# Running sums of squares of all norms: from VectorE to GpSimd

## The chip, the cores and the metric

The kernel runs on one core of a Trainium2 chip. Its metric is the device time of one execution in microseconds (us), the median of several runs. The engines of the core work side by side, each through its own instruction list in order: TensorE (PE in the trace; PEld is its weight load), VectorE (DVE), ScalarE (ACT), GpSimd (POOL) and SyncE (SP, which issues the DMA transfers). An instruction starts when the one before it on its engine has been issued and when the semaphores it waits for have been raised.

## What is computed

One inference step of a hybrid backbone of two layers on 640 tokens (512 latent, 128 context) with 1024 channels. Each layer is FFN, token mixer, FFN; the mixer of the first layer is differential attention, that of the second a gated linear recurrence (HGRN). Every sub-layer normalises its input and its output and adds the result to the residual stream:

```python
def rmsnorm(x, g):
    xf = x.astype(jnp.float32)
    y = xf * lax.rsqrt(jnp.mean(xf * xf, axis=-1, keepdims=True) + EPS)
    return (y * g.astype(jnp.float32)).astype(x.dtype)
def ada_pre(x, mod, j, g):
    return rmsnorm(x, g) * (1 + scale) + shift
def ada_post(x, y, mod, j, g, res_w):
    return x + res_w * gate * rmsnorm(y, g)
def swiglu(h, w_in, w_out):
    a, b = jnp.split(h @ w_in, 2, axis=-1)
    return (jax.nn.silu(a) * b) @ w_out
def ffn_sublayer(x, mod, j, g_pre, g_post, w_in, w_out):
    return ada_post(x, swiglu(ada_pre(x, mod, j, g_pre), w_in, w_out), mod, j, g_post, 0.5)
```

scale, shift and gate are rows of a modulation that is computed from a conditioning vector with matmuls of their own. So six sub-layers hold twelve norms, each over 640 tokens.

## The kernel before

**Layout.** Activations stand with channels on partitions: X, Y and H are arrays of eight tiles of 128 channels by 640 tokens. The tokens are in two groups, 0 and 1, of NG = 320, and each norm is done for each group apart: twelve norms by two groups make 24 norm sums. Most matmuls are 128x128 weights against 320 tokens. Values and weights are split into a high and a low part, whl and H (index 0 and 1), and three products make up one (lines 452, 457 and 484); ScalarE writes the high part of a weight (line 360), VectorE the low one (line 362).

**A norm.** `square` (lines 545 to 556) squares one tile on ScalarE: the first tile's squares are written into the group's running sum acc (line 552), the others into a tile sq of two buffers (line 555), and the function that it returns adds sq to acc (line 556). There are seven such adds for each norm sum. When all eight tiles are in, `stat_mm` (line 522) multiplies acc by ones on TensorE, which sums over the partitions; `token_rstd` and `rsqrt` (lines 529 and 507 to 517) compute the reciprocal root in 13 small instructions on VectorE; `token_spread` (line 534) brings it back to all partitions with matmuls by the identity.

**Who calls it.** At the startup, X is transposed on TensorE (line 855), copied (line 858) and squared tile by tile for both groups; then follow the modulation rows (matmuls of line 763, ScalarE's copy of line 873, matmuls of line 724, VectorE's lines 733 and 748) and the first normalised input. At the end of a sub-layer, `y_part` adds the last part of the output product to a tile of Y (line 1132) and squares it; its add is put into a list (`self.later`), from which the loop over matmul jobs takes one at its next step. `post_gen` does the post norm of a group: the sum, then per tile nt = Y times gate times root (line 573), X += nt (line 579) and the square of X, whose add comes one step later. `pre_gen` sums these squares and writes the normalised input: nt (line 606), the high part of H on ScalarE (line 611), the low part on VectorE (line 619). Both are generators that `run_jobs` steps between the matmuls of the jobs, so that one group's norm runs beside the other group's matmuls. The very last post norm writes the output (`last_out`).

**What sets the order.** The program is written out as above, and the scheduler of the language then places each engine's instructions by its own estimate of when they can run. A change of one instruction's engine therefore moves others on all engines. Each sub-layer's end and the next one's start are called a joint here: A, FFN to attention; B, attention to FFN; C, FFN to FFN of the next layer; D, FFN to HGRN; E, HGRN to FFN. In each joint there are four norm sums, in this order: post norm of group 0, pre norm of group 0, post norm of group 1, pre norm of group 1.

Of the kernel before, what the change touches and what calls it, by code (L numbers as in the profile page):

```python
# [14 lines left out]
ALU = mybir.AluOpType  # L15
# [203 lines left out]
class Net:  # L219
# [328 lines left out]
    def square(self, g, src, first):  # L548
        nc = self.nc
        acc = self.acc[g]  # L550
        if first:
            nc.scalar.activation(out=acc, in_=src, func=AF.Square)
            return lambda: None
        sq = self.np_.tile([128, NG], F32, name="sq", tag="sq", bufs=2)
        nc.scalar.activation(out=sq, in_=src, func=AF.Square)  # L555
        return lambda: nc.vector.tensor_tensor(out=acc, in0=acc, in1=sq, op=ALU.add)  # L556

    def post_gen(self, l, j, g, ps, squares):
        nc = self.nc
# [1168 lines left out]
```

## Time and profile before

| | |
|---|---|
| median of 3 runs | 2783.96 us (2780.76 to 2785.59) |
| the profiled execution's own time | 2780.47 us |
| its span in the profile | 2778.7 us |
| mean granted TensorE clock | 0.990 |
| busy: TensorE, VectorE, ScalarE, GpSimd | 98%, 71%, 47%, 0% of the span |
| the 168 adds of line 556 | 80.1 us on VectorE |

The span runs from the first to the last instruction that the profiler recorded; the time has in addition what lies around it. A row of the timeline has the start and the duration in us, the engine, the line, the operation, what is written and read, how many instructions are merged, and in brackets the idle time before it with what ended that. A duration covers the whole of an instruction, and the next one on the same engine can start before it ends. A row of windows has the busy time of each engine in a stretch with the number of instructions, the granted clock of TensorE as a share, the DMA engines' share and GB/s. A wait row has the total, the times and the longest.

### The profile page before, as it was taken

The numbers are of one execution on the slowest core, as the hardware profiler recorded it, in microseconds if no ns is written. First come the engines' busy times: TensorE is split into PE (matmuls) and PEld (weight loads), VectorE is DVE, ScalarE is ACT, GpSimd is POOL, SyncE is SP. The second block draws the span as 40 slices with busy tenths as digits, with TensorE's granted clock in tenths as the row PEclk, the third lists the DMA queues.
The fourth block names the chain that finished last, engine by engine and source line by source line (L and its number), as shares of the span: only waits on it lengthen the run. The fifth ranks groups of instructions, "written<-read, shape, count | busy, mean of one in ns | idle before, by whom it ended". The sixth has DMA issues, their size and how long they took to land.

```text
span 2778.7 us, 47467 instructions
## 1 busy us (share of the span) xinstructions
PE 2715.6 (98%) x18670; PEld 2613.1 (94%) x18670; DVE 1977.8 (71%) x4285; ACT 1307.3 (47%) x2693; POOL 0.2 (0%) x4
## 2 busy tenths in 40 slices
PE   7999999899999999999999999999999999999998
PEld 5999999899998999999999999999999999999997
DVE  6766676887777965667786657687677678867574
ACT  4443444476675553435354434443343345545363
POOL 0000000000000000000000000000000000000000
PEclk9999999999999999999999999999999999999999
DMA  9556224211122456524244442421221222323231
GB/s 305 176 192 198 81 77 145 60 53 54 46 74 75 161 161 201 165 81 145 69 143 132 142 145 77 137 78 35 61 58 50 60 65 93 90 77 90 78 122 54
DMA packets 426077, 299.10 MB, mean 108 GB/s; under 512 B 9051, under 2 KB 386429, under 8 KB 424829
## 3 DMA queue, kind: packets, MB, share of 16 engines
q1 hardware_dynamic: 425344, 295.86, 34.6%
q8 instruction: 147, 2.41, 0.4%
q14 instruction: 78, 0.63, 0.1%
q10 hardware_dynamic: 508, 0.20, 0.0%
HBM read 280.82 MB, written 15.20 MB: 107 GB/s over the span
## 4 chain that ended last, share of the span: by engine, by line
PE 89%; DVE 5%; ACT 4%; DMA 1%; issue 1%; ACTq 0%; DVEq 0%; SPq 0%
PE mmps L484 31%; PE mmps L452 30%; PE mmps L457 15%; PE aux L1564 2%; PE aux L763 2%; PE mmps L1403 1%; DVE whl L362 1%; PE aux L1372 1%; ACT p L1302 1%; PE aux L1373 1%; PE aux L522 1%; PE aux L1601 1%; PE aux L534 1%; ACT whl L360 1%; ACT sq L1635 0%
## 5 line engine op out<-in xcount | busy, mean ns | idle before, releaser
L360 ACT ACTIVATE whl<-wraw 128x512 fp32r<-128x512 f32 (+4 forms) x644 | 464.2, 722 | 661.3 <-PE mmps L452 369.6
L362 DVE TENSOR_TENSOR whl<-wraw,whl 128x512 fp32r<-128x512 f32 (+4 forms) x644 | 515.3, 801 | 207.8 <-ACT whl L360 199.6
L452 PE MATMUL mmps<-H,whl 128*128 128x320 f32 x2624 | 571.5, 317 | 9.3 <-ACT H L611 6.9
L484 PE MATMUL mmps<-H,whl 128*128 128x320 f32 x3456 | 544.1, 309 | 0.1
L484 PEld LDWEIGHTS mmps<-H,whl 128*128 128x128 f32 x3456 | 515.3, 188 | 10.5 <-issue 4.2
L452 PE MATMUL mmps<-G,whl 128*128 128x320 f32 x2448 | 487.7, 311 | 3.8 <-ACT G L1649 1.5
L452 PEld LDWEIGHTS mmps<-H,whl 128*128 128x128 f32 x2624 | 432.5, 191 | 19.5 <-ACT H L611 8.3
L452 PEld LDWEIGHTS mmps<-G,whl 128*128 128x128 f32 x2448 | 391.2, 188 | 13.7 <-issue 5.9
L457 PE MATMUL mmps<-H,whl 128*128 128x320 f32 x1312 | 369.6, 314 | 0.7 <-DVE whl L362 0.7
L484 PE MATMUL mmps<-T,whl 128*128 128x320 f32 x2160 | 352.5, 309 | 0.0
L484 PEld LDWEIGHTS mmps<-T,whl 128*128 128x128 f32 x2160 | 325.4, 188 | 5.0 <-issue 2.5
L457 PE MATMUL mmps<-G,whl 128*128 128x320 f32 x1224 | 304.9, 310 | 0.0
L457 PEld LDWEIGHTS mmps<-H,whl 128*128 128x128 f32 x1312 | 239.1, 191 | 1.1 <-DVE whl L362 1.0
L457 PEld LDWEIGHTS mmps<-G,whl 128*128 128x128 f32 x1224 | 211.4, 188 | 0.0
L452 PE MATMUL mmps<-G,H 128*128 128x320 f32 x880 | 198.7, 312 | 0.1
L1132 DVE TENSOR_TENSOR Y<-Y,mmps 128x320 f32<-128x320 f32 x208 | 94.8, 482 | 127.8 <-PE mmps L457 127.6
L452 PEld LDWEIGHTS mmps<-G,H 128*128 128x128 f32 x880 | 147.8, 189 | 0.3 <-ACT Y L1130 0.3
L457 PE MATMUL mmps<-G,H 128*128 128x320 f32 x440 | 137.3, 312 | 0.0
L452 PE MATMUL mmps<-H,G 128*128 128x320 f32 x448 | 103.5, 312 | 0.0
L997 ACT ACTIVATE sa<-sa 128x320 f32<-128x320 f32 x144 | 67.9, 471 | 66.4 <-DVE sa L1000 65.5
L135 DVE TENSOR_TENSOR s<-wraw 128x512 f32<-128x512 f32 x72 | 49.7, 690 | 69.0 <-DMA wraw<-in_ffn_w_in 68.9
L556 DVE TENSOR_TENSOR acc<-acc,sq 128x320 f32<-128x320 f32 x168 | 80.1, 485 | 22.1 <-ACT sq L555 21.2
(260 smaller groups left out, 3572.5 us busy)
## 6 DMA issues: line engine op xcount, KB each, us to landing
wraw<-in_ffn_w_in SPq DMA_DIRECT2D x192, 512.0 KB, 4.3
wmod<-in_w_mod SPq DMA_DIRECT2D x66, 1024.0 KB, 7.1
wraw<-in_hgrn_w_in SPq DMA_DIRECT2D x40, 512.0 KB, 3.9
wraw<-in_ffn_w_out SPq DMA_DIRECT2D x32, 448.0 KB, 3.7
wraw<-in_ffn_w_out SPq DMA_DIRECT2D x32, 384.0 KB, 3.3
wraw<-in_attn_w_in SPq DMA_DIRECT2D x24, 512.0 KB, 3.8
xs<-X SPq DMA_DIRECT2D x4, 2560.0 KB, 12.8
wraw<-in_ffn_w_out SPq DMA_DIRECT2D x32, 320.0 KB, 3.2
```

The costliest lines, as they stand in the source:

```text
L135: V.tensor_tensor(out=z, in0=a[:, lo], in1=b[:, lo], op=ALU.subtract)
L360: nc.scalar.activation(out=u.w[0][:, 0:nk, :], in_=src, func=AF.Copy)
L362: self.los.append(lambda: nc.vector.tensor_tensor(out=u.w[1][:, 0:nk, :], in0=src, in1=u.w[0][:, 0:nk, :].bitcast(F32), op=ALU.subtract))
L452: nc.tensor.matmul(out=ps[g][:, 0:NG], lhsT=w[0][:, a, :], rhs=rhs[:, r, b, g * NG:(g + 1) * NG], start=(i == 0 and r == 0), stop=False,)
L457: nc.tensor.matmul(out=ps[g][:, 0:NG], lhsT=w[1][:, a, :], rhs=rhs[:, 0, b, g * NG:(g + 1) * NG], start=False, stop=(i == last),)
L484: nc.tensor.matmul(out=ps[:, 0:NG], lhsT=w[a][:, k, :], rhs=j.operand(r, k), start=(j.first and k == 0 and n == 0), stop=(k == 3 and n == ...
L522: self.nc.tensor.matmul(out=ps[:, c0 + n:c0 + n + 1], lhsT=acc[:, b0:b0 + 128], rhs=self.ones, start=True, stop=True,)
L556: return lambda: nc.vector.tensor_tensor(out=acc, in0=acc, in1=sq, op=ALU.add)
L763: self.nc.tensor.matmul(out=ps[g * 32:(g + 1) * 32, 0:512], lhsT=CS[:, k, 30 - 2 * i:62 - 2 * i], rhs=ts[half][:, g, :], start=first and h ...
L997: A.activation(out=e[name], in_=e[name], func=AF.Silu)
L1132: nc.vector.tensor_tensor(out=y, in0=y, in1=ps, op=ALU.add)
L1564: nc.tensor.matmul(out=ps[:, c * 128:(c + 1) * 128], lhsT=km[:, c * 128:(c + 1) * 128], rhs=self.view(Q2, c * 128, dims), start=True, stop ...
```

## The change

The add of line 556 is issued on GpSimd instead of VectorE, in all its 168 places. Operands and buffers are the same.

```diff
         sq = self.np_.tile([128, NG], F32, name="sq", tag="sq", bufs=2)
         nc.scalar.activation(out=sq, in_=src, func=AF.Square)
-        return lambda: nc.vector.tensor_tensor(out=acc, in0=acc, in1=sq, op=ALU.add)
+        return lambda: nc.gpsimd.tensor_tensor(out=acc, in0=acc, in1=sq, op=ALU.add)
```

The instruction lists of all engines come out in another order. Three places show how; acc_95 and acc_96 are the running sums of groups 0 and 1, Y_82 and Y_103 the outputs of groups 0 and 1.

TensorE at the startup, before, from the last modulation rows (wm_143, wm_144 are their weights) to the first matmuls of the first FFN:

```order
L763 MATMUL mmps<-wm_143,CS 32x512 x4
L522 MATMUL aux<-ones,acc_95 128x1 x3
L522 MATMUL aux<-ones,acc_96 128x1 x3
L763 MATMUL mmps<-wm_144,CS 32x512 x4
L724 MATMUL mmps<-sel,Y_82 128x4 x4
L534 MATMUL aux<-ident,rs_y 128x128 x2
L534 MATMUL aux<-ident,rs_y 128x64
L534 MATMUL aux<-ident,rs_y 128x128 x2
L534 MATMUL aux<-ident,rs_y 128x64
L452 MATMUL mmps<-H,whl 128x320 x3
```

and now:

```order
L763 MATMUL mmps<-wm_140,CS 32x512 x4
L522 MATMUL aux<-ones,acc_95 128x1 x3
L522 MATMUL aux<-ones,acc_96 128x1 x3
L763 MATMUL mmps<-wm_143,CS 32x512 x4
L534 MATMUL aux<-ident,rs_y 128x128 x2
L534 MATMUL aux<-ident,rs_y 128x64
L534 MATMUL aux<-ident,rs_y 128x128 x2
L534 MATMUL aux<-ident,rs_y 128x64
L763 MATMUL mmps<-wm_144,CS 32x512 x4
L724 MATMUL mmps<-sel,Y_82 128x4 x4
```

The four rows of spreads (L534), which stood last, now stand ahead of the modulation rows of wm_144 and the L724 matmuls, and wm_143 has moved behind the two sums.

VectorE in joint A, the update of X for group 0, as a piece of the difference:

```order
 L573 SCALAR_TENSOR_TENSOR nt<-Y_82,POST,aux 128x320
 L579 TENSOR_TENSOR X<-X,nt 128x320
-L556 TENSOR_TENSOR acc_95<-acc_95,sq 128x320
-L556 TENSOR_TENSOR acc_96<-acc_96,sq 128x320
 L573 SCALAR_TENSOR_TENSOR nt<-Y_82,POST,aux 128x320
 L579 TENSOR_TENSOR X<-X,nt 128x320
-L556 TENSOR_TENSOR acc_95<-acc_95,sq 128x320
 L573 SCALAR_TENSOR_TENSOR nt<-Y_82,POST,aux 128x320
 L579 TENSOR_TENSOR X<-X,nt 128x320
```

and GpSimd in joint A, now:

```order
L556 TENSOR_TENSOR acc_95<-acc_95,sq 128x320 x8
L556 TENSOR_TENSOR acc_96<-acc_96,sq 128x320
L556 TENSOR_TENSOR acc_95<-acc_95,sq 128x320 x5
L556 TENSOR_TENSOR acc_96<-acc_96,sq 128x320
L556 TENSOR_TENSOR acc_95<-acc_95,sq 128x320
L556 TENSOR_TENSOR acc_96<-acc_96,sq 128x320 x12
```

VectorE keeps L573 and L579 and has no instruction between a tile's update and the next tile's L573; GpSimd has the adds, those of the two groups one after the other in one list (seven of group 0's post norm and the first of its pre norm are the x8). Ahead of the very first add, at the startup, its list has one instruction more, an ISA row of the same line.

TensorE in joint A around the sum of the post norm of group 1, before (G is the activation that the last product of the FFN reads, or a buffer of weights):

```order
L452 MATMUL mmps<-G,H 128x320 x2
L457 MATMUL mmps<-G,H 128x320
L522 MATMUL aux<-ones,acc_96 128x1 x3
L534 MATMUL aux<-ident,rs_y 128x128 x2
L534 MATMUL aux<-ident,rs_y 128x64
L452 MATMUL mmps<-H,whl 128x320 x3
L452 MATMUL mmps<-H,G 128x320
L452 MATMUL mmps<-H,whl 128x320
```

and now:

```order
L452 MATMUL mmps<-H,whl 128x320 x2
L457 MATMUL mmps<-H,whl 128x320
L452 MATMUL mmps<-H,whl 128x320 x2
L457 MATMUL mmps<-H,whl 128x320
L452 MATMUL mmps<-H,whl 128x320 x3
L457 MATMUL mmps<-H,whl 128x320
L452 MATMUL mmps<-H,whl 128x320
L522 MATMUL aux<-ones,acc_96 128x1 x3
L457 MATMUL mmps<-H,whl 128x320
L452 MATMUL mmps<-H,whl 128x320 x2
L457 MATMUL mmps<-H,whl 128x320
```

The sum stood behind the last matmuls of the old FFN and ahead of the first ones of the attention's input product (H on the left); now 14 matmuls of that product stand ahead of it.

Counted over the whole list, this many 320-column matmuls stand ahead of each norm sum on TensorE, before and now:

| joint | post, group 0 | pre, group 0 | post, group 1 | pre, group 1 |
|---|---|---|---|---|
| A | 2796, 2795 | 2914, 2892 | 2952, 2966 | 3072, 3072 |
| B | 4314, 4307 | 4420, 4392 | 4502, 4506 | 4635, 4602 |
| C | 7284, 7283 | 7395, 7367 | 7444, 7457 | 7567, 7577 |
| D | 10236, 10235 | 10354, 10332 | 10392, 10405 | 10523, 10531 |
| E | 12532, 12519 | 12647, 12600 | 12712, 12714 | 12863, 12810 |

The two sums of the last post norm have 15492 and 15648 matmuls ahead of them before, 15491 and 15648 now.

## Rows read from the trace of the kernel before

**Rows 1.** The page: span, busy time, the costliest groups.
```profile
span 2778.7 us, 47467 instructions
...
PE 2715.6 (98%) x18670; PEld 2613.1 (94%) x18670; DVE 1977.8 (71%) x4285; ACT 1307.3 (47%) x2693; POOL 0.2 (0%) x4
...
L362 DVE TENSOR_TENSOR whl<-wraw,whl 128x512 fp32r<-128x512 f32 (+4 forms) x644 | 515.3, 801 | 207.8 <-ACT whl L360 199.6
...
L556 DVE TENSOR_TENSOR acc<-acc,sq 128x320 f32<-128x320 f32 x168 | 80.1, 485 | 22.1 <-ACT sq L555 21.2
```

**Rows 2.** Timeline, a dense stretch on TensorE.
```profile
143.12 1.92 PE L484 MATMUL mmps<-T,whl 128*128 128x320 f32 x12
...
144.88 1.92 PE L484 MATMUL mmps<-H,whl 128*128 128x320 f32 x12
```

**Rows 3.** Windows: the five joints A to E.
```profile
476.00:556.00 80.00, 71.86 (x456) 70.09 (x456) 65.44 (x194) 35.62 (x70) 0.00 (x0) 0.91 0.18 53
856.00:936.00 80.00, 79.86 (x541) 77.85 (x541) 70.36 (x198) 42.98 (x86) 0.00 (x0) 0.99 0.32 105
1326.00:1406.00 80.00, 78.04 (x518) 73.62 (x517) 66.13 (x193) 33.99 (x69) 0.00 (x0) 0.98 0.36 112
1790.00:1870.00 80.00, 76.22 (x511) 74.25 (x509) 65.46 (x188) 37.31 (x72) 0.00 (x0) 0.98 0.23 66
2270.00:2360.00 90.00, 85.21 (x568) 82.75 (x567) 74.57 (x218) 45.63 (x99) 0.00 (x0) 0.98 0.24 77
```

**Rows 4.** Waits of TensorE: line, releaser, total us, times, longest.
```profile
PE mmps L452 <- ACT H L611: 6.9, 6, 2.0
...
PE aux L522 <- DVE acc L556: 3.9, 2, 2.3
```

**Rows 5.** Timeline, joint A: the last add and sum, post norm, group 0.
```profile
482.82 0.49 DVE L556 TENSOR_TENSOR acc<-acc,sq 128x320 f32<-128x320 f32 x1 [0.60 <-ACT sq L555]
...
483.45 0.80 PE L522 MATMUL aux<-ones,acc 128*128 128x1 f32 x6
```

**Rows 6.** Timeline, the first memsets of GpSimd and VectorE.
```profile
0.23 0.10 POOL L1715 MEMSET const-float32-0.0<- 128x1 f32 x1 [0.23 <-issue]
...
0.80 0.06 DVE L828 MEMSET ones<- 128x1 f32 x1 [0.80 <-PEq L1715]
```

**Rows 7.** Timeline, joint B: the X update of group 0 on VectorE.
```profile
874.08 0.48 DVE L579 TENSOR_TENSOR X<-X,nt 128x320 f32<-128x320 f32 x1
874.48 0.48 DVE L556 TENSOR_TENSOR acc<-acc,sq 128x320 f32<-128x320 f32 x1
...
875.34 0.48 DVE L579 TENSOR_TENSOR X<-X,nt 128x320 f32<-128x320 f32 x1
```

**Rows 8.** Timeline, the startup.
```profile
15.79 0.46 ACT L555 ACTIVATE sq<-X 128x320 f32<-128x320 f32 x1
...
25.35 1.91 DVE L556 TENSOR_TENSOR acc<-acc,sq 128x320 f32<-128x320 f32 x4
...
27.00 1.88 PE L522 MATMUL aux<-ones,acc 128*128 128x1 f32 x12 [2.27 <-DVE acc L556]
...
31.46 1.87 PE L724 MATMUL mmps<-sel,Y 128*128 128x4 f32 x8 [0.72 <-ACT Y L873]
...
33.19 2.80 PE L534 MATMUL aux<-ident,rs_y 128*128 128x128 f32 x12
...
35.50 1.46 DVE L606 SCALAR_TENSOR_TENSOR nt<-X,PRE,aux 128x320 f32<-128x320 f32 x3
```

**Rows 9.** Timeline, joint A: the sum of the post norm, group 1.
```profile
511.14 0.80 PE L522 MATMUL aux<-ones,acc 128*128 128x1 f32 x6 [2.35 <-DVE rs_y L517]
```

**Rows 10.** Timeline, joint E: adds and sum, post norm, group 0.
```profile
2280.91 0.48 DVE L556 TENSOR_TENSOR acc<-acc,sq 128x320 f32<-128x320 f32 x1
...
2284.11 1.67 DVE L556 TENSOR_TENSOR acc<-acc,sq 128x320 f32<-128x320 f32 x3
...
2286.06 0.72 PE L522 MATMUL aux<-ones,acc 128*128 128x1 f32 x6
```

## The prediction

> **What bounds the kernel now.** I read the page first: TensorE is busy 98% of the span, VectorE 71%, GpSimd not at all; the running sums are 168 adds on VectorE, 80.1 us, 485 ns each [rows 1]. In the dense parts TensorE issues twelve 320-column matmuls every 1.76 us, 0.147 us each [rows 2], and nothing on VectorE matters there. The change can count only where TensorE waits for a norm. So I cut the five joints between sub-layers out by windows: A (FFN to attention), B (attention to FFN), C (FFN to FFN), D (FFN to HGRN), E (HGRN to FFN) [rows 3]. TensorE is idle there for 8.1, 0.1, 2.0, 3.8 and 4.8 us, and in A its granted clock is 0.91. Nineteen us, and the startup, is all that is to be had. The waits of TensorE name the owners: H, that is the normalised input, 6.9 us, and the running sum 3.9 us in two waits [rows 4]. Then the timeline at single norm sums: in A the last add ends at 482.82 + 0.49 = 483.31 and the ones-matmuls start at 483.45 [rows 5], 0.14 us later. The instruction order holds almost no slack there against a slower add, and the order itself is written anew by the change (rows in the section on the change).
>
> **The price of one add on GpSimd.** The trace has no GpSimd arithmetic. Lower bound: VectorE's own 0.485 us [rows 1]. Upper bound: GpSimd's small memset takes 0.10 us against VectorE's 0.06 [rows 6], a ratio of 1.67, so 0.81 us; with one VectorE instruction of 0.40 us (start to start, as from 874.08 to 874.48 [rows 7]) in its way, 1.2 us. I take 1.0, between 0.81 and 1.2, because the only row of GpSimd against VectorE is the memset, which holds mostly fixed cost. Call the price c. The Trainium skill, "GPSIMD Engine Reference", section "Performance versus the Vector engine", gives about 2.6 cycles per element for an add of two inputs where VectorE takes 1, and 4497 against 2293 ns at 2048 columns: an estimate of 0.95 us by that ratio, with which the sum below would be about 1 us lower; no run here shows it yet.
>
> **The change, part by part.** Removed: 168 VectorE adds, 0.40 us each where they are back to back. Added: the same adds on GpSimd, and one extra GpSimd instruction ahead of the first of them (an ISA row). GpSimd has about 15 us of nothing before the first square is there at 15.79 [rows 8], so I cost that row at nothing; whatever it took beyond that would be added to the startup.
>
> Startup: **+6**. Before, the last of 14 adds ends at 25.35 + 1.91 = 27.26, and the sums follow from 27.00 (group 0's add is done earlier). Now the adds can start when the first square ends, 15.79 + 0.46 = 16.25, and GpSimd is through at 16.25 + 14 x 1.0 = 30.25: +3. The new order also puts the four spreads (L534) ahead of the last modulation matmuls (L763) and the L724 group, which before ran while VectorE computed the reciprocal roots. From L724's start at 31.46 to the first nt at 35.50 were 4.0 us [rows 8], most of which now stands behind the spreads: about +3. At c = 0.485 ScalarE's squares, not the adds, would end last, some 4 us earlier than 27.26, and +3 for the order minus some of that leaves +2 or a little less; at c = 1.2 the adds end at 33.05, +5.8, and the order's +3 makes +9. Bounds +2 to +9.
>
> Joints. In the X update VectorE runs nt (L573), X (L579) and add (L556) per tile with a period of 1.26 us (874.08 to 875.34 [rows 7]). Without the add it is 0.86, so GpSimd with c = 1.0 becomes the bound, but the loop still ends some 2.8 us (7 x 0.40) less the longer last add (1.0 - 0.485 = 0.5) earlier: +2.3 of relief. The new order spends more than this: the pre-norm sum of group 0 stands 22, 28, 28, 22 and 47 matmuls earlier on TensorE in A to E, and VectorE's relief doesn't cover it. Each: matmuls x 0.147 - 2.8 + 0.5. And the post-norm sum of group 1 stands 14, 13 and 13 matmuls later in A, C and D, which fills idle time with H matmuls.
> - A: the wait of 2.35 us at group 1's sum [rows 9] gets 14 x 0.147 = 2.1 us of matmuls ahead of it, part of the second wait for H and of the lost clock come back (about 2), group 0's sum loses 22 x 0.147 - 2.3 = 0.9: **-3** (-4.6 to -1.5).
> - B: no idle time to fill. 28 x 0.147 - 2.3 = 1.8 and, for group 1, 33 x 0.147 - 2.3 = 2.6: **+4** (+1 if group 1 profits of both reliefs, +8 if VectorE's other work takes them up).
> - C: 28 matmuls cost 1.8, 13 give back at most the idle 2.0 and a little clock: **-0.5** (-3 to +2.5).
> - D: 22 cost 0.9, 13 give 1.9 and some of the remaining 1.9 idle: **-2** (-4 to +0.5).
> - E: the squares of the last Y tiles come in a burst. Seven adds went from 2280.91 to 2285.78 on VectorE, the sum at 2286.06 [rows 10]; on GpSimd seven take 7.0 from about 2280.7, to 2287.7: 1.9 later, while TensorE arrives 13 matmuls, 1.9 us, earlier. That wait of up to 3.8 partly overlaps the 4.8 us that are idle today; group 0's pre sum, 47 - 13 = 34 further matmuls early, costs 2.7: **+4** (-0.5 to +7).
>
> Post-norm sums after A to D and the end: the last add is 0.5 longer and 0.14 of slack goes against it [rows 5], and TensorE arrives one matmul earlier, so about 0.5 each, five of them: **+2** (+0.3 to +3).
>
> SyncE's queue changes place in a few rows (the spill of X and some weight loads); each moves by a handful of loads in queues that are used to 34.6% of their time, and TensorE's waits [rows 4] show no weight load: nothing, or up to 1 us if a spill delays a load. ScalarE issues the same squares; sq has two buffers, so a square waits for the add two before it. ScalarE is busy 44% in A [rows 3]: its delay is covered as long as the wait is about one add.
>
> Sum: 6 - 3 + 4 - 0.5 - 2 + 4 + 2 = **+10.5** on the profiled execution, whose 2780.47 us is 3.5 below the median of the runs, 2783.96. Forecast 2794.5 for the median. All low ends together make -8.8, all high ends +28.5 (+29.5 with a late load); they won't fall together at the high side, where c and VectorE's other work both have to be bad.
>
> **The rivals.** R1, faster: adds are cheap, c of 0.8 or less, and nothing hinders VectorE. Then the X loops are bound by VectorE's 0.86 us, every add is done before the next square comes, and joints A, C and D give up most of their 14 us of idle time. Terms at their low ends are -8.8; not all reach them, and I take -7, that is 2777. For it: VectorE at 82% in A, 88% in B [rows 3] is truly scarce there. Against: it must beat the earlier places of the sums. The point is c about 0.8 to 0.9.
>
> R2, slower still: GpSimd and VectorE hinder each other. If an add excludes VectorE's instructions that take both inputs from SBUF (L579, L619, L362), the X loop has a period of 1.26 - 0.40 + 1.0 = 1.86, 8 x 0.6 = 4.8 us longer, 2.0 after the 2.8 of relief that the order counts on. Five sums of group 0 show it whole, five of group 1 half (H matmuls of group 0 cover the rest): 15 us in place of the joints' +2.5, with startup and ends 6 + 2 + 15 = +23: 2807. For it: L362 alone is 515 us of VectorE, 801 ns each [rows 1], and runs through every joint. Against: the trace of before can't show it. The Trainium skill, "SBUF — State Buffer", section "Who interferes with whom", states just such a lock for the pair of ports that both engines share, held for a whole instruction; no run here shows it yet.
>
> R3, no change: relief and earlier sums cancel in each joint, the startup hides behind the first weight loads: +2, 2786.
>
> R4 would be that the change does nothing it says; the order shows the 168 adds on GpSimd, so it gets no chance.
>
> **How the numbers follow.** Forecast 0.38 (2788 to 2799), R1 0.26 (2772 to 2781), R2 0.21 (2800 to 2815), R3 0.15 (2782 to 2788). About 0.2%, 5.6 us, is what a measurement of this kernel can tell from no change. Faster by more (under 2778.4): three quarters of R1, 0.20. Within: R3, the rest of R1, and a fifth of the forecast's own range (below 2789.5), 0.15 + 0.06 + 0.07 = 0.28. Slower: 0.31 + 0.21 = 0.52. The range 2775 to 2812 leaves out the bottom of R1 (a third of it, 0.09) and the top of R2 (0.06), and holds the rest.
>
> **What would show it.** The price: the mean of L556 on GpSimd, 1.0 by the forecast, under 0.85 by R1. The hindrance: L579 on VectorE longer than 0.48, or L556 with two lengths, beside each other (R2). The startup: the first nt at 41 to 42 rather than 35.50. The joints: TensorE's busy time in windows of the same matmuls, more idle in B and E, less in A and D; waits of TensorE at L522 for the GpSimd sum. I am wrong if L556 is near 1.0 and B and E are as dense as before, if A, C and D gain more than 9 us together, or if the startup moves by less than 2 us.

## The result and the profile after

The changed kernel takes 2827.06 us (median of 4 runs, 2825.79 to 2830.80), the kernel before in the same session 2783.05 us (4 runs): a ratio of 1.0165, 95% interval 1.0153 to 1.0178, or +44.0 us. The forecast was slower, +10.5 us, with 2812 as the upper end. The sign was right, the size was not. The profiled execution took 2825.79 us with a span of 2824.0, against 2780.47 and 2778.7 [rows 1]: +45.3 us.

The page of the changed kernel, its span, busy times and the group of the adds:

```profile
span 2824.0 us, 47631 instructions
...
PE 2725.8 (97%) x18670; PEld 2623.5 (93%) x18670; DVE 1938.0 (69%) x4117; ACT 1308.9 (46%) x2693; POOL 166.1 (6%) x172
...
L556 POOL TENSOR_TENSOR acc<-acc,sq 128x320 f32<-128x320 f32 x168 | 165.9, 996 | 2645.9 <-ACT sq L555 2641.1
```

The adds now stand on GpSimd, 996 ns each. VectorE has lost 39.8 us of busy time, not the 80.1 us that its adds took [rows 1]. TensorE is busy for 10.2 us more with the same 18670 matmuls, and idle for the remaining 35.1 us of the 45.3.

The waits of TensorE, as line, releaser, total us, times and longest:

```profile
PE aux L522 <- POOL acc L556: 46.5, 23, 5.2
...
PE mmps L452 <- ACT H L611: 3.1, 2, 1.8
```

The first row alone is more than the 35.1 us that TensorE is idle longer. Of 24 norm sums 23 now wait for GpSimd's last add, 46.5 us in all, where two waited for 3.9 us before [rows 4]. The wait for H has shrunk from 6.9 to 3.1 us: TensorE loses its time earlier in the chain.

The five joints A to E by windows (busy us of PE, PEld, DVE, ACT and POOL with counts, clock, DMA share, GB/s):

```profile
476.00:556.00 80.00, 67.83 (x419) 65.60 (x419) 54.71 (x156) 30.72 (x62) 24.94 (x25) 0.88 0.16 46
856.00:936.00 80.00, 65.81 (x418) 63.70 (x419) 52.51 (x139) 35.52 (x69) 29.91 (x28) 0.91 0.30 96
1326.00:1406.00 80.00, 74.73 (x489) 72.78 (x488) 52.36 (x122) 31.23 (x54) 21.20 (x22) 0.96 0.42 126
1790.00:1870.00 80.00, 75.15 (x503) 73.93 (x503) 50.25 (x110) 34.15 (x58) 20.41 (x21) 0.98 0.40 122
2270.00:2360.00 90.00, 79.67 (x537) 77.94 (x536) 59.10 (x136) 35.92 (x75) 19.78 (x20) 0.94 0.17 49
```

Joint B, as dense as could be before (79.86 of 80 us [rows 3]), has 14 us of idle time, and the granted clock there fell from 0.99 to 0.91. (The changed kernel reaches each joint later, B by 10 and E by 33 us, so of these rows A and B compare best.)

In place of windows that drift, the start of the same matmul was read in each trace and the difference taken; between two such marks lies what a joint costs. In us, against the kernel before:

| | startup | A | B | C | D | E | last norm |
|---|---|---|---|---|---|---|---|
| predicted | +6 | -3 | +4 | -0.5 | -2 | +4 | in the +2 for sums |
| changed kernel | +3.6 | +6.7 | +11.8 | +8.1 | +2.6 | +11.2 | +1.2 |
| VectorE's adds, new order | +3.4 | +3.4 | +8.5 | +2.0 | +0.1 | +9.0 | -0.1 |
| GpSimd's adds, old order | +0.9 | +0.9 | +2.4 | +1.3 | +2.2 | +3.4 | +1.3 |
| one column, new order | -0.3 | -4.6 | +4.1 | -4.1 | -5.8 | -2.0 | 0.0 |
| one column, old order | -4.5 | -0.9 | -0.3 | -0.4 | -0.5 | -2.4 | +0.2 |

(Marks: matmuls 1000, 2700 to 3700, 3700 to 5200, 7200 to 9200, 10200 to 12200, 12450 to 14500 of the 15648 with 320 columns. The last four rows belong to experiments below.)

TensorE's longer busy time comes from four of the joints. Between these marks it is busy for 2.3, 1.6, 2.9 and 2.2 us more in A, B, C and E, where the granted clock fell from 0.970 to 0.956, 0.989 to 0.979, 0.995 to 0.979 and 0.995 to 0.984. In D it is busy for 0.2 us more, and the clock stayed at 0.996.

How the time goes in one joint is seen in B, the X update of group 0 and its norm sum, on the timeline of the changed kernel:

```profile
881.84 0.49 DVE L579 TENSOR_TENSOR X<-X,nt 128x320 f32<-128x320 f32 x1
882.65 11.66 POOL L556 TENSOR_TENSOR acc<-acc,sq 128x320 f32<-128x320 f32 x10 [8.47 <-ACT sq L555]
882.70 0.49 DVE L579 TENSOR_TENSOR X<-X,nt 128x320 f32<-128x320 f32 x1
...
883.56 0.72 DVE L579 TENSOR_TENSOR X<-X,nt 128x320 f32<-128x320 f32 x1
883.96 0.47 ACT L555 ACTIVATE sq<-X 128x320 f32<-128x320 f32 x1 [0.56 <-POOL acc L556]
...
884.65 0.70 DVE L579 TENSOR_TENSOR X<-X,nt 128x320 f32<-128x320 f32 x1
...
885.74 1.79 DVE L579 TENSOR_TENSOR X<-X,nt 128x320 f32<-128x320 f32 x2
...
887.46 3.69 DVE L362 TENSOR_TENSOR whl<-wraw,whl 128x1024 fp32r<-128x1024 f32 x2
...
893.55 1.44 PE L522 MATMUL aux<-ones,acc 128*128 128x1 f32 x6 [5.24 <-POOL acc L556]
```

GpSimd's list holds ten adds in a row, seven of X and three of the other group's Y: 11.66 us, 1.17 each. The last add of X is the ninth; it ends as TensorE's sum starts. The L579 at 881.84, with no add beside it, takes 0.49 us as before [rows 7]. The one at 882.70, which starts with the first add, takes 0.49 too, and that add takes 1.27; the four after it, which start while GpSimd adds, take 0.70 to 0.72 and the last 1.16. Two weight conversions (L362) take 3.69 us in place of some 2.4. TensorE stands at the sum for 5.24 us.

How long L579 and L573 took over the whole run (ns, least, median and most; L573 has one of its inputs in PSUM), before:

```profile
L579 DVE TENSOR_TENSOR X<-X,nt x88: 475/482/487, 490.5 to 2744.5; 128x320 f32<-128x320 f32 x88
...
L573 DVE SCALAR_TENSOR_TENSOR nt<-Y,POST,aux x128: 333/406/548, 489.6 to 2743.3; 128x320 f32<-128x320 f32 x48, 128x192 f32<-128x192 f32 x40, 128x128 f32<-128x128 f32 x40
```

and in the changed kernel, with the adds themselves:

```profile
L579 DVE TENSOR_TENSOR X<-X,nt x88: 476/576/1165, 494.6 to 2788.8; 128x320 f32<-128x320 f32 x88
...
L573 DVE SCALAR_TENSOR_TENSOR nt<-Y,POST,aux x128: 331/411/549, 493.7 to 2787.5; 128x320 f32<-128x320 f32 x48, 128x192 f32<-128x192 f32 x40, 128x128 f32<-128x128 f32 x40
...
L556 POOL TENSOR_TENSOR acc<-acc,sq x168: 851/879/1832, 15.5 to 2811.4; 128x320 f32<-128x320 f32 x168
```

L573 is as it was; L579, both of whose inputs are in SBUF, goes up to 1165 ns. An add takes 0.86 us in the mean where VectorE has nothing beside it (57 adds), 0.87 beside others, most of them with an input in PSUM (23), and 1.11, up to 1.83, beside L579, L362 or L619 (88).

At the startup the order costs what was forecast, and the adds nothing:

```profile
15.47 11.52 POOL L556 TENSOR_TENSOR acc<-acc,sq 128x320 f32<-128x320 f32 x14 [15.03 <-ACT sq L555]
...
26.23 2.72 PE L522 MATMUL aux<-ones,acc 128*128 128x1 f32 x12 [3.48 <-POOL acc L556]
...
31.10 2.82 PE L534 MATMUL aux<-ident,rs_y 128*128 128x128 f32 x12 [0.29 <-DVE rs_y L517]
...
36.15 1.05 PE L724 MATMUL mmps<-sel,Y 128*128 128x4 f32 x8 [0.73 <-ACT Y L873]
...
37.85 1.47 DVE L606 SCALAR_TENSOR_TENSOR nt<-X,PRE,aux 128x320 f32<-128x320 f32 x3
```

Fourteen adds take 11.52 us, 0.82 from start to start, and end at 26.99, where VectorE's ended at 27.26 [rows 8]; the forecast had 30.25. The new order (spreads ahead of L724) brings the first nt to 37.85 instead of 35.50, where 41 to 42 was forecast.

### The profile page after: what moved, and what is told of

It is laid out like the page before. It is cut to its first block, busy times and chain, and to the rows that moved or that the text cites. A ratio compares the mean times of both kernels' runs of the same rounds, so it can differ in the third digit from the quotient of the medians.

```text
span 2824.0 us, 47631 instructions
## 1 busy us (share of the span) xinstructions
PE 2725.8 (97%) x18670; PEld 2623.5 (93%) x18670; DVE 1938.0 (69%) x4117; ACT 1308.9 (46%) x2693; POOL 166.1 (6%) x172
## 4 chain that ended last, share of the span: by engine, by line
PE 84%; DVE 6%; ACT 4%; POOL 4%; issue 1%; DMA 1%; ACTq 0%; DVEq 0%; POOLq 0%; SPq 0%
PE mmps L484 31%; PE mmps L452 27%; PE mmps L457 13%; POOL acc L556 4%; PE aux L1564 2%; PE aux L763 2%; PE mmps L1403 1%; DVE whl L362 1%; PE aux L522 1%; PE aux L1372 1%; ACT whl L360 1%; ACT p L1302 1%; PE aux L534 1%; PE aux L1373 1%; PE aux L1601 1%
## 5 line engine op out<-in xcount | busy, mean ns | idle before, releaser
L362 DVE TENSOR_TENSOR whl<-wraw,whl 128x512 fp32r<-128x512 f32 (+4 forms) x644 | 521.4, 811 | 207.5 <-ACT whl L360 200.1
L484 PEld LDWEIGHTS mmps<-H,whl 128*128 128x128 f32 x3456 | 515.2, 188 | 10.2 <-issue 4.2
L556 POOL TENSOR_TENSOR acc<-acc,sq 128x320 f32<-128x320 f32 x168 | 165.9, 996 | 2645.9 <-ACT sq L555 2641.1
L452 PE MATMUL mmps<-G,H 128*128 128x320 f32 x880 | 206.7, 322 | 0.1
L452 PEld LDWEIGHTS mmps<-G,H 128*128 128x128 f32 x880 | 154.9, 197 | 0.3 <-ACT Y L1130 0.3
L457 PE MATMUL mmps<-G,H 128*128 128x320 f32 x440 | 141.2, 321 | 0.0
```

Of the source, the lines that this page charges most:

```text
L362: self.los.append(lambda: nc.vector.tensor_tensor(out=u.w[1][:, 0:nk, :], in0=src, in1=u.w[0][:, 0:nk, :].bitcast(F32), op=ALU.subtract))
L452: nc.tensor.matmul(out=ps[g][:, 0:NG], lhsT=w[0][:, a, :], rhs=rhs[:, r, b, g * NG:(g + 1) * NG], start=(i == 0 and r == 0), stop=False,)
L457: nc.tensor.matmul(out=ps[g][:, 0:NG], lhsT=w[1][:, a, :], rhs=rhs[:, 0, b, g * NG:(g + 1) * NG], start=False, stop=(i == last),)
L484: nc.tensor.matmul(out=ps[:, 0:NG], lhsT=w[a][:, k, :], rhs=j.operand(r, k), start=(j.first and k == 0 and n == 0), stop=(k == 3 and n == ...
L556: return lambda: nc.gpsimd.tensor_tensor(out=acc, in0=acc, in1=sq, op=ALU.add)
```

## Experiments: the order or the engine

Two things changed at once, the engine of the adds and the order of everything. A table of instruction numbers with issue-order edges (no semaphore, no wait) pins the order of TensorE, VectorE and ScalarE, so that each could be had without the other. The edit, the same in all runs that say "pinned":

```diff
+def pin(tc):
+    import base64, json, zlib
+    at = {i.name: i for i in tc.nc.cur_bb.bb.instructions}
+    for ns in json.loads(zlib.decompress(base64.b85decode(ORDER))).values():
+        ns = [f"I-{n}" for n in ns if f"I-{n}" in at]
+        for a, b in zip(ns, ns[1:]):
+            tc.add_manual_dep(
+                at[b], a, mybir.DependencyInfo(mybir.DependencyClass.NoSync, mybir.DependencyReason.DATA),
+                reason="pin",
+            )
...
         net.finish()
+        pin(tc)
```

**GpSimd's adds in the old order** (the changed kernel, pinned to the order before):

> The adds run on GpSimd, but a table pins the instruction order of TensorE, VectorE and ScalarE to that of the kernel before. Theory O (the new order is to blame: TensorE meets its norm sums 22 to 53 matmuls, 3 to 8 us, earlier than before): most of the +44 us is gone, +5 to +15 us over the kernel before. Theory E (the adds themselves are to blame: they take 0.85 to 1.8 us, and they stretch VectorE's additions to X): +30 us or more stays, because the last add before each of the 24 sums is late in either order.

2791.64 us against 2782.94: ratio 1.0032 (1.0021 to 1.0043), +8.7 us.

**VectorE's adds in the new order** (the kernel before, pinned to the order of the changed one):

> The mirror image: the adds run on VectorE, the order of the three engines is pinned to that of the changed kernel. Theory O: +25 to +40 us, TensorE waits at the sums for VectorE's adds nearly as long as for GpSimd's. Theory E: within 10 us of the kernel before; the sums wait for 1 us or less.

2806.69 us: ratio 1.0084 (1.0069 to 1.0099), +23.7 us. The waits at the sums, of the first run and then of the second:

```profile
PE aux L522 <- POOL acc L556: 12.6, 14, 3.0
```

```profile
PE aux L522 <- DVE acc L556: 28.5, 16, 3.0
```

Theory O holds for the larger part: the same GpSimd adds cost 8.7 us in the old order and 44 in the new one. But the new order with VectorE's adds costs 23.7, just under that theory's band, and its sums wait for 28.5 us, not nearly the 46.5 of the changed kernel. The two together cost 12 us more than the sum of each by itself. Neither cause alone tells the story.

**Which part of the order.** In two further runs less was pinned. Only the 22 norm sums behind the startup, each held behind the matmul that stood ahead of it before:

```diff
+    for a, b in SUMS:
+        tc.add_manual_dep(
+            at[f"I-{a}"], f"I-{b}", mybir.DependencyInfo(mybir.DependencyClass.NoSync, mybir.DependencyReason.DATA),
+            reason="pin",
+        )
```

> The changed kernel, in which only the norm sums on TensorE are held back: each may not be issued before the matmul that stood ahead of it in the kernel before; all else is the scheduler's. Theory P (of the new order, the place of the sums is what costs): within 8 us of the kernel with the whole old order, +5 to +16 us over the kernel before. Theory Q (what VectorE and ScalarE do in another order costs): +25 us or more.

2794.79 us against 2782.33: ratio 1.0045 (1.0030 to 1.0060), +12.4 us. Theory P: 22 edges take back 32 of the 44 us, together with what the scheduler then moved (VectorE's and ScalarE's lists differ from both earlier ones). Then the whole list of TensorE alone:

> Adds on GpSimd, TensorE's whole order pinned to that of the kernel before, VectorE and ScalarE free. Theory P: +4 to +12 us, as with all three pinned, or a little less, since VectorE's order now makes use of the time that the adds leave. Theory Q: +25 us or more.

2803.13 us: ratio 1.0073 (1.0056 to 1.0090), +20.8 us, a miss for both. TensorE's old list with VectorE and ScalarE in another order is worse than the sums alone; why was not followed up. It is also 12 us worse than the same list of TensorE and the same adds with all three orders old (+8.7), so the order of VectorE and ScalarE counts by itself.

With the five pre-norm sums of group 0 ten matmuls later still:

> As the run in which only the sums are held back to their old places, but the five pre-norm sums of group 0 stand 10 matmuls (1.5 us) later still. If TensorE only came too early, its waits at these five sums go and the time falls by 2 to 5 us against that run, to +7 to +10 us over the kernel before. If the whole chain behind the sum (root, spread, H) is what TensorE waits for in the end, the waits move to the spreads and H, and the time stays within 3 us of that run.

2789.18 us against 2781.33: ratio 1.0026 (1.0017 to 1.0035), +7.9 us, in the band of the first case. The waits at L522 fall from 18.6 to 13.8 us, those at the spreads (L534) rise from 6.0 to 9.2: some of the time only moves on. No place of the sums that was tried reaches the kernel before.

## Experiments: the lock

The next edit puts work beside VectorE that nobody needs. VectorE keeps its adds:

```diff
+            nc.vector.tensor_tensor(out=acc, in0=acc, in1=sq, op=ALU.add)
+            nc.gpsimd.tensor_tensor(out=junk, in0=sq, in1=sq, op=ALU.add)
```

> The adds that count stay on VectorE; beside each of the 154 that follow the startup and the 14 of it GpSimd adds sq to itself into a scratch tile that nobody reads. The number of matmuls ahead of each sum is that of the kernel before. Theory L (GpSimd and VectorE shut each other out while both work on two inputs from SBUF): VectorE's adds and its L579 go from 0.48 us to 0.7 and more wherever a scratch add runs, each X update ends 2 to 4 us later, +15 to +30 us in all. Theory S (only the slowness of a GpSimd add that TensorE waits for counts): L579 stays at 0.48 us, and the time moves by less than 4 us.

2826.92 us against 2782.94: ratio 1.0148 (1.0129 to 1.0167), +44.0 us, above the band of either theory. The lists of TensorE, VectorE and ScalarE are those of the kernel before, instruction for instruction. So that GpSimd should not hold sq either, a second form, in which each scratch add starts when a square (`ins`) has ended:

```diff
-            nc.gpsimd.tensor_tensor(out=junk, in0=sq, in1=sq, op=ALU.add)
+            own = nc.gpsimd.tensor_tensor(out=junk, in0=junk, in1=junk, op=ALU.add)
+            self.tc.add_manual_dep(
+                getattr(own, "ins", own), getattr(ins, "ins", ins).name,
+                mybir.DependencyInfo(mybir.DependencyClass.Sync, mybir.DependencyReason.DATA), reason="own",
+            )
```

> The kernel before with the same order on TensorE, VectorE and ScalarE; beside it GpSimd adds a tile of its own to itself, 168 times, each started when a square ends. Nobody waits for these adds and they hold no buffer of the others. If it was the lock that cost 44 us in the run with sums of sq, it costs 30 to 45 us here too, and VectorE's additions to X start or end later wherever GpSimd runs. If it was sq, which GpSimd's reading held back from ScalarE, under 10 us.

2826.35 us against 2781.33: ratio 1.0152 (1.0135 to 1.0169), +45.0 us. Here GpSimd shares no data with anyone, and nobody waits for it. Joint B on its timeline (L594 is the addition to X, L564 VectorE's add, L565 GpSimd's):

```profile
882.26 0.48 DVE L594 TENSOR_TENSOR X<-X,nt 128x320 f32<-128x320 f32 x1
...
888.60 0.72 POOL L565 TENSOR_TENSOR gj<-gj 128x320 f32<-128x320 f32 x1 [1.06 <-ACT sq L557]
888.67 0.99 DVE L594 TENSOR_TENSOR X<-X,nt 128x320 f32<-128x320 f32 x1
889.59 0.48 DVE L564 TENSOR_TENSOR acc<-acc,sq 128x320 f32<-128x320 f32 x1
...
890.38 0.72 POOL L565 TENSOR_TENSOR gj<-gj 128x320 f32<-128x320 f32 x1 [1.06 <-ACT sq L557]
890.45 0.99 DVE L594 TENSOR_TENSOR X<-X,nt 128x320 f32<-128x320 f32 x1
```

L594 starts 0.07 us after GpSimd's add and takes 0.99 us: the 0.65 that are left of GpSimd's 0.72, and then most of its own 0.48. The period of a tile is 1.78 us (888.67 to 890.45) where it was 1.26 [rows 7]. Over the run L594's mean rises from 482 to 620 ns (88 times) and that of VectorE's adds from 485 to 636 (168 times). TensorE's work in this run, and its wait at the sums (L524):

```profile
PE 2735.2 (97%) x18670; PEld 2629.4 (93%) x18670; DVE 2022.9 (72%) x4285; ACT 1308.2 (46%) x2693; POOL 154.3 (5%) x173
```

```profile
PE aux L524 <- DVE acc L564: 27.1, 14, 4.7
```

So the mere presence of GpSimd costs 45 us, nearly all of it in two parts. At the sums TensorE waits 27.1 us for VectorE's adds, where it waited 3.9 before; and with the same list it is busy for 19.6 us more (2735.2 against 2715.6), at a granted clock of 0.983 where it was 0.990. The mechanism of R2 is shown. The Trainium skill, "SBUF — State Buffer", section "Who interferes with whom", says that an instruction of VectorE with two inputs in SBUF contends with one of GpSimd that reads SBUF, by an exclusive lock on the ports that they share, and that one with at most one SBUF input, outside the 2-port modes, does not. The trace agrees in both halves: L594 here and L579 above are held up, and L573, with one input in PSUM, is not.

**Buffers of sq.** In the changed kernel ScalarE waits 34.0 us in 56 waits for GpSimd to give back a buffer of sq:

```profile
ACT sq L555 <- POOL acc L556: 34.0, 56, 1.3
```

With a third buffer (the same edit at all four places where sq is made), all orders pinned to the new one:

```diff
-        sq = self.np_.tile([128, NG], F32, name="sq", tag="sq", bufs=2)
+        sq = self.np_.tile([128, NG], F32, name="sq", tag="sq", bufs=3)
```

> The changed kernel with three buffers of sq instead of two, all three orders pinned to those of the changed kernel. If ScalarE's squares that wait for GpSimd to give a buffer back (34 us in 56 waits) stand on the path, 8 to 20 us less than the changed kernel. If the path is X, square, add, each after the other, within 4 us of it.

2827.40 us: ratio 1.0164 (1.0149 to 1.0179), the same as the changed kernel, although those waits fell to:

```profile
ACT sq L555 <- POOL acc L556: 14.8, 24, 1.3
```

They were not on the path.

**nt in PSUM**, so that L579 has one input in SBUF only, with GpSimd's adds and, as the control, with VectorE's. X is then also updated in the step that makes nt, not one step later:

```diff
+        t = ps[:, 8:8 + NG]
...
-                nc.vector.tensor_tensor(out=x, in0=x, in1=ts.pop(i - 1), op=ALU.add)
+                nc.vector.tensor_tensor(out=x, in0=x, in1=t, op=ALU.add)
```

> As the changed kernel, but nt of the X update (L573) is written to PSUM, so that L579 reads only one operand from SBUF; the scheduler then also puts the sums of group 0's pre norm near their old places on TensorE. Theory L: L579 stays at about 0.48 us beside an add, the adds there take 0.86 rather than 1.0 to 1.1, and the X updates end about 2 us earlier: 15 to 25 us less than the changed kernel. Theory S: adds of 0.85 and the same waits at the post-norm sums, at most 6 us less.

> The control for the run with nt in PSUM: the same X update, but the adds on VectorE. If nt in PSUM costs by itself (L579 must wait for L573, and the order is new), +15 to +30 us over the kernel before, and GpSimd's adds without the lock are then worth -5 to +10. If it costs nothing, within 5 us of the kernel before, and the 30 us of the other run are GpSimd's.

2812.91 us (ratio 1.0104, 1.0089 to 1.0119) and 2807.74 us (1.0092, 1.0077 to 1.0107). The addition to X (L578 in these kernels) stays at 420 to 489 ns beside GpSimd's adds, so the lock on it is gone. GpSimd's adds cost some 4 us over their control (+30.0 against +26.4) instead of 44, and the whole is 14 us less than the changed kernel, just under the expected band. But the control itself is 26 us slower than the kernel before, and the sums stand at other places in both lists, so this pair bears the lock out and does not measure it.

## Experiments: the price, and where the adds sit

Which squares cost, in the old order. Only those of X on GpSimd (70 adds), then only those of Y (84). `square` gets the engine as an argument and takes VectorE without it; the edit for X, that for Y is the same at its own call:

```diff
-                    adds[i - 1] = self.square(g, x, i == 1)
+                    adds[i - 1] = self.square(g, x, i == 1, nc.gpsimd)
```

> In the old order of all three engines, only the 70 adds of the squares of X go to GpSimd; those of Y and of the startup stay on VectorE. If the lock and the late last add stand against the time that VectorE saves in the X loop, they are about even: -2 to +5 us. If the lock is the whole of the +9 us of the full move, +7 to +9.

> In the old order, only the 84 adds of the squares of Y go to GpSimd. They run beside instructions that read PSUM and are mostly alone, 0.86 us each; only the last one of a sum counts: 0.4 us longer by 11 sums, +3 to +6 us; with the burst in the joint from HGRN to FFN 2 us of it. If only the lock costs, 0 to +2.

X: 2785.27 us against 2782.33, ratio 1.0010 (1.0001 to 1.0020), +2.9; Y: 2789.94, ratio 1.0026 (1.0015 to 1.0038), +7.6. In the old order the lock does not decide: the X adds meet it (the addition to X takes up to 1164 ns) and cost 2.9 us. That the time which VectorE saves nearly pays for them fits this but was not measured by itself. The Y adds cost somewhat more than was expected; TensorE waits for them 8.3 us at ten sums.

What remained open was why VectorE's saved time does not pay for the early sums of the new order: is the order bad, or the adds too dear for it? The changed kernel with the new order pinned, and only a part of each add's columns: one, as here, then `0:160`, then one in the old order. The other columns are left out of the sums.

```diff
-        return lambda: nc.gpsimd.tensor_tensor(out=acc, in0=acc, in1=sq, op=ALU.add)
+        return lambda: nc.gpsimd.tensor_tensor(out=acc[:, 0:1], in0=acc[:, 0:1], in1=sq[:, 0:1], op=ALU.add)
```

> The changed kernel in its own order, pinned, with each GpSimd add cut to 1 of 320 columns (319 columns of each square but the first are left out of the sums): an add that costs next to nothing and locks next to nothing. If the order is right for cheap adds and only the real price and the lock spoil it, the time is at or below the kernel before, -20 to +3 us. If the order is bad by itself, as its +24 us with VectorE's adds could mean, +10 us or more.

> The same with 160 of 320 columns (half of each square but the first is left out): about half the price of an add and half the lock. If price and lock are what counts, about half way between the run with one column and the changed kernel. If a fixed cost of crossing to GpSimd and back counts, near the changed kernel, +35 us or more.

> One column of each add on GpSimd, in the old order of the three engines: what the saving on VectorE is worth where TensorE's list is not changed. If VectorE bounds the joints, -10 us or more (the idle time of joint A and half of that of D and E). If TensorE's list is as dense as it can be, -5 to 0.

One column in the new order: 2770.63 us against 2781.00, ratio 0.9959 (0.9944 to 0.9974), -10.4 us, in the band of its first case. Half the columns: 2788.31, ratio 1.0026 (1.0015 to 1.0036), +7.3, a third of the way to the changed kernel rather than half. One column in the old order: 2773.69, ratio 0.9975 (0.9966 to 0.9985), -7.3, between its two cases. TensorE's work, the adds and the waits of the first:

```profile
PE 2705.4 (98%) x18670; PEld 2605.1 (94%) x18670; DVE 1915.4 (69%) x4117; ACT 1307.2 (47%) x2693; POOL 51.1 (2%) x172
...
L556 POOL TENSOR_TENSOR acc<-acc,sq x168: 186/192/1755, 16.0 to 2754.5; 128x1 f32<-128x1 f32 x168
L579 DVE TENSOR_TENSOR X<-X,nt x88: 480/486/494, 489.9 to 2731.9; 128x320 f32<-128x320 f32 x88
...
PE aux L522 <- POOL acc L556: 8.0, 9, 1.4
```

and of the second:

```profile
L556 POOL TENSOR_TENSOR acc<-acc,sq x168: 514/532/3449, 15.0 to 2774.5; 128x160 f32<-128x160 f32 x168
L579 DVE TENSOR_TENSOR X<-X,nt x88: 476/486/848, 491.0 to 2751.9; 128x320 f32<-128x320 f32 x88
...
PE aux L522 <- POOL acc L556: 20.0, 18, 3.5
```

All of it in one table, us against the kernel before of the same session:

| the adds | price of one, us (median; mean, new order) | old order | new order |
|---|---|---|---|
| GpSimd, 1 column | 0.19; 0.30 | -7.3 | -10.4 |
| GpSimd, 160 columns | 0.53; 0.66 | not run | +7.3 |
| VectorE, 320 columns | 0.48; 0.49 | 0 | +23.7 |
| GpSimd, 320 columns | 0.88; 1.00 | +8.7 | +44.0 |

The new order is not bad. With adds that cost next to nothing it is no worse than the old one: 3 us better, less than single runs of one kernel differ by. By the marks its joints are 8 us better than those of the old order and its startup 4 us worse. Most of what the cheap adds win is TensorE's clock: the profiled execution is 12.2 us shorter than that of the kernel before, and 10.2 of them are busy time (2705.4 against 2715.6), at a granted clock of 0.994 where it was 0.990.

The new order counts on early sums, and each 0.1 us that an add is dearer is multiplied: from 0.19 to 0.53 us the time rises by 17.7 us, 52 us per us of price. On that line, which has two points, the plain price of 0.88 us would give +26, an estimate. The other 18 us would then be the lock, which half an add meets less (the median of L579 is 486 ns there, though the adds' mean is 0.66 us and one took 3.45). No run holds the lock and the price apart in the new order, so this split stays an estimate.

## Why the prediction was wrong

**What held.** The place: the joints' norm sums, with E and B the worst. The price of an add, 1.0 us, measured 0.996 in the mean, but by luck in part: it was set from a memset, and the 0.996 is a mixture of 0.86 alone and 1.11 beside instructions that lock. (The Trainium skill's ratio in "GPSIMD Engine Reference", section "Performance versus the Vector engine", gave an estimate of 0.95, which lies between the two.) At the startup the +3 for the order held (+3.4 with VectorE's adds in the new order, +3.6 in the changed kernel); the +3 for the adds did not, for GpSimd was through at 26.99 and not at 30.25. The mechanism of R2, which had a chance of 0.21, held too.

**The step that failed** is the relief of the joints: "the loop still ends some 2.8 us (7 x 0.40) less the longer last add (1.0 - 0.485 = 0.5) earlier: +2.3 of relief". Joint B from the post-norm sum of group 0 to its pre-norm sum, before:

```profile
863.22 0.72 PE L522 MATMUL aux<-ones,acc 128*128 128x1 f32 x6
...
877.41 0.48 DVE L579 TENSOR_TENSOR X<-X,nt 128x320 f32<-128x320 f32 x1
...
879.75 0.88 DVE L556 TENSOR_TENSOR acc<-acc,sq 128x320 f32<-128x320 f32 x2
...
880.51 0.72 PE L522 MATMUL aux<-ones,acc 128*128 128x1 f32 x6
```

In the changed kernel this stretch starts at the row below; its last L579 and its pre-norm sum stand in the timeline of B above.

```profile
874.24 0.83 PE L522 MATMUL aux<-ones,acc 128*128 128x1 f32 x6 [1.39 <-POOL acc L556]
```

VectorE did get a relief: counted from the post-norm sum, its last L579 ends 0.3, 1.4, 2.0, 0.9 and 1.6 us earlier in A to E. But the last add of X ends later: at 18.2, 17.0, 17.3, 18.0 and 17.8 us before, at 19.6, 19.3, 17.9, 19.6 and 19.8 now. That is 1.6 later in the mean where the forecast had it 2.3 earlier. From sum to sum it is 18.9, 17.3, 17.9, 18.9 and 18.5 us before and 19.7, 19.3, 17.9, 19.7 and 19.9 now. The loop was costed with VectorE's work alone, although the prediction itself had called GpSimd the bound; at its 1.0 us per tile seven tiles give only 7 x 0.26 = 1.8, less 0.5. And GpSimd's list was not counted out: in each joint nine adds stand in it from the first of X to the last, two of them the other group's. They take 9.7 to 10.8 us, at 1.06 to 1.18 each. The lock, put into R2 as an alternative, belonged into the forecast's own loop once c was 1.0, for then GpSimd is adding nearly all the time that L579 runs.

Without relief the formula of the prediction is close. Matmuls that no longer stand ahead of the sum, by 0.147 us: 3.2, 4.1, 4.1, 3.2 and (34 in E) 5.0; the idle time ahead of these five sums: 3.6, 5.2, 3.8, 3.6 and 4.9 us.

**The terms beside it.** From joint A to the end the forecast's terms add up to +4.5 us, and the two traces differ by 41.6. Group 0's pre-norm sums wait for 21.1 us, where their five terms make 8.1: 13 us. Group 1's pre-norm sums wait for 2.7, 2.2, 2.5, 1.1 and 2.2 us, 10.8 in all, and only B's had a term, 2.6: 8 us. The post-norm sums wait for 11 us, where 1.3 of E's +4 and the +2 had been set (five times 0.5 would have been 2.5): 8 us. The credits for filled idle time in A, C and D, 9 us, came in idle time: besides these waits TensorE is idle for 10.7 us less than it was in all before. They were eaten by a term that the forecast did not have, the clock. TensorE is busy for 9.4 us more with the same matmuls at a lower granted clock, where the forecast had even counted on some clock coming back in A: 8 us net. In the runs with one column, where the clock rose, the credits show (A -4.6, C -4.1, D -5.8).

**R2's price** was too low, +23 against +44: its 15 us were put "in place of the joints' +2.5", when a lost relief adds to the early sums that the formula had already paid for with it. Its 2.0 per sum also takes off the 2.8 of relief once more, though its period of 1.86 us no longer holds VectorE's add. **R1** described a kernel that exists: with cheap adds and no hindrance the new order does bring -10.4 us, where R1 said -7. Its condition, c of 0.8 or less, was not enough; at 0.53 us the time is already above the kernel before.

**The order as a cause of its own.** The prediction read the new places of the sums off the lists, rightly, but took them as a small cost that a relief pays for. They were the lever: this order gains only with adds far cheaper than these, and TensorE's list is fixed, so each sum that comes too early is a wait. None of the runs with whole adds points to a version that beats the kernel before; the best of them is X alone in the old order, +2.9 us.

## What to carry to other kernels

Before work is moved to an idle engine, count that engine's whole list in the stretch that matters, in its own order, with the price of each instruction beside what runs there; relief on the old engine is worth nothing past the point where the new list becomes the longer one. Where a scheduler orders the program, a changed engine is a changed order: pin the old order with the new engine and the new order with the old engine, and the two causes come apart in two runs. An engine that helps can cost by its mere presence: a scratch instruction that nobody reads, placed beside the old work, measures that directly. And TensorE's busy time belongs beside its waits: with the same matmuls it was 10 us shorter to 20 us longer in these runs, with the granted clock.

## What the runs showed that was not expected

168 adds of GpSimd on a tile of its own cost 45 us, as much as the whole change. Longer times also showed in instructions that read one tile of SBUF, beside an add: an L510 of 128x3 in the root, 173 ns at most before, took 828 once in the changed kernel, and two L1468 of 128x320 took 993 and 1024, where 443 was the most before. An add of one column takes 0.19 us on GpSimd, one of 160 columns 0.53 and one of 320 columns 0.88, about 2.1 ns per column over a fixed 0.19. And 22 issue-order edges, with no wait of their own, were worth 32 us of the 44, with what the scheduler moved for them.
